# The forget gates' small logarithm chain on GpSimd, and the loads of the state-space tables on GpSimd's queue

## The chip, the cores and the metric

One Trainium2 chip; the kernel runs on one core of it. The metric is device time in microseconds (us) of one execution. Engines are named as in the profile: PE (TensorE, matmuls; PEld is its weight load), DVE (VectorE), ACT (ScalarE), POOL (GpSimd), SP (SyncE, which here only issues DMAs). An engine's name with a q (SPq, POOLq) is its instruction queue. L1820 is line 1820 of the kernel.

## The reference

Two transformer-like blocks on 512 tokens of 1024 features in float32. The change touches the token mixers of the second block, of which there are two (one per layer), and a helper that the first block uses once.

```python
def token_mixer(h, w_in, forget_b, ...):
    u, q, k, v, f, g_a, g_b = jnp.split(h @ w_in, cuts, axis=-1)
    y_ssm = s5_ssm(u, ...)                      # 32 groups of 16 features, 64 complex states each
    z_val, z_gate = jnp.split(gelu(y_ssm) @ glu_w, 2, axis=-1)
    y_a = z_val * sigmoid(z_gate)
    y_b = forgetting_attention(q, k, v, f + forget_b) @ attn_w_out   # 8 heads of 64
    return (sigmoid(g_a) * y_a + sigmoid(g_b) * y_b) @ w_out

def forgetting_attention(q, k, v, f_logit):
    cum = cumsum(log_sigmoid(f_logit), axis=1)   # 512 tokens x 8 heads
    s = q k^T / 8 + (cum_t - cum_s), causal; softmax; @ v
```

The logarithm that the diff touches is `log_sigmoid(x) = min(x, 0) - log(1 + exp(-|x|))`; `log(1 + e)` is a polynomial of `s = e / (2 + e)`.

## The kernel before

Products are taken in three parts (high x high, high x low, low x high) of float32 values split by ACT (L122, the high part) and DVE (L125, the low part). Weights come from DRAM as raw units (tile `wr`, at most 1 MB, two buffers), issued by SP at L132 in the order of the program; ACT and DVE split a unit into `wh` and `wl`, and PE uses it. A unit's DMA can be issued when the raw buffer that it takes has been split.

The instructions of SP stay in program order. Those of PE, DVE and ACT do so in the stages that are written out by hand (`down` and `up`; in the attention PE's alone); elsewhere, and for POOL everywhere, a planner at build time orders each engine's instructions by program order and by when it expects them to be ready. On the chip each engine executes its list in order, and waits at an instruction that isn't ready.

A mixer runs in this order:

1. The end of the feed-forward layer before it: `down`, the norms of four tiles of 128 tokens (each takes two POOL instructions, L294 and L297), transposes (tile `tp`, L340) and the first three blocks of the mixer's own projections, whose sums make `u`.
2. The scan stage, `ssm`. Sixteen tiles of states s, four for each feature tile j. For each s: products of the inputs with the table `b` (L1842, `bu`), a turn, a scan and a turn back on DVE (L1857 to L1875, which gives `st_x`), products with the tables `k` and `c` (L1878 and L1880, `st`), and four copies by ACT (L1882). Between them PE works on fourteen products of the gates (tile `gab`, L214 to L216), one after each of the first ten s, each unit of weights feeding two; ACT takes their sigmoid and stores it (L2076, L2077: `sga`, `pair`).
   `load(j)` fetches what feature tile j takes: four DMAs for `b` (128 KB each, L1820), one for `sc` (512 KB, L1821), four for `k` (tile `st_k`, 16 to 64 KB, L1824) and one for `c` (512 KB, L1825), ten in all, from DRAM, where the layers before have put them. Each tile has two buffers. `load(0)` is called ahead of the loop and `load(j + 1)` at the first s of j; after it `inputs(j + 1)` issues sixteen copies of `u` on POOL (L1834). The calls stand ahead of the next `take()` of weights in the program, so on SP they stand ahead of the weights' DMAs.
3. The attention. PE in this order: values of heads 4 to 7 with the forget logits f, queries and keys of the first two heads (`qk`), values of heads 0 to 3 (`v`, four token tiles in three PSUM buffers), the cumulative sum (`cum`, L1913, of `f_lf` with the triangle `tri`), then the heads one by one. `forget_logs` (L1899 to L1905) turns f into `f_lf`: tiles of 128 x 32, two ACT instructions (L1900, L1901) and 26 DVE instructions, most of them in `log1p` (L1063 to L1071).

The DMA of POOL's queue are generated by software; SP's and ACT's are the hardware kind (q1, q10 in the profile).

Of the kernel before, what the change touches and what calls it, by code (L numbers as in the profile page):

```python
# [44 lines left out]
class Builder:  # L45
# [14 lines left out]
    # ---------------------------------------------------------------- helpers  # L60
# [5 lines left out]
    def ring(self):  # L66
        """Room for two units of weights, for good."""
        p = self.late.enter_context(self.pool("weights", side="right"))
        self.wp, self.nw, self.used, self.kept = [p, p, None], 2, [0, 1, 2], []

    @contextmanager
    def third(self, side):
        """Room for a third unit."""
        with self.pool("third", side=side) as self.wp[2]:
            self.nw = 3
            yield
            self.nw = 2

    @contextmanager
    def psum_pool(self, **tags):  # L80
        """PSUM by tags: how many pairs of banks each; in a tag that ends in 1, single banks."""
        with self.tc.tile_pool(name="psum", bufs=1, space=PSUM, reuse_waits="tile") as p:
            old = getattr(self, "ps", None)
            self.ps = (p, tags)
            yield p
            self.ps = old
# [24 lines left out]
    def pair(self, name, tag):  # L111
        """Two banks that engines may use at the same time."""
# [5 lines left out]
    def split(self, src, h, l, eng="act"):  # L118
        """h + l = src exactly, both of twelve significant bits."""
# [7 lines left out]
    def load_w(self, pieces, n, chunks=1):  # L127
        """Stage one unit of weights (n words a partition); the function returned splits it."""
# [18 lines left out]
    def stage_cols(self, w, cols, k0=0, k1=None, chunks=1, dmas=1):  # L147
        """Columns of w (lists of (start, width)) for the row tiles k0..k1; a function gives them split, [p, k, column]."""
# [21 lines left out]
    def feed(self, units):  # L170
        """Queue functions that stage weights (or pairs of a name and a function), in the order of their use by take()."""
        self.units += [u if isinstance(u, tuple) else ((), u) for u in units]

    def take(self, *name, keep=False, hold=False):
        """The next queued weights; the ones after them come on their way (but for hold)."""
# [10 lines left out]
    def advance(self, keep=False):  # L186
        """Have two units ready or in work, if there is room beside those kept."""
# [9 lines left out]
    def stage(self, n):  # L197
        """Have n units of weights on their way."""
# [4 lines left out]
    def poke(self, n=1):  # L203
        """Split n parts of the weights that come next."""
# [13 lines left out]
    def fm(self, ps, wh, wl, c, kts=KD, xh=None, xl=None, t=slice(0, S), ks=None):  # L218
        """ps = w[:, c].T @ x, features x tokens (of the sum over kts tiles, those in ks)."""
# [9 lines left out]
    def tok(self, x, k, tt):  # L229
        """Features k x the tokens of tile tt."""  # L230
        return x[:, tt // 2, k, tt % 2 * P:(tt % 2 + 1) * P]

    def bg(self, steps=1, psum=True):
        """Advance the queued side work by some steps (without PSUM: what does not ask for PE next)."""
# [16 lines left out]
    # ---------------------------------------------------------------- setup  # L251
# [17 lines left out]
    def consts(self, part):  # L269
        """The constants that the first norm takes, or the others."""  # L270
# [13 lines left out]
    # ---------------------------------------------------------------- norms  # L284
    def norm_scale(self, srcs, junk, which):
        """1 / sqrt(mean(x ** 2) + eps) for each row of x, in one piece or in two."""
# [13 lines left out]
    def post_add(self, tt, acc, grow, out=None):  # L300
        """x[tt] += grow * acc / rms(acc), to out too; a generator of three stages."""
# [25 lines left out]
    def pre_steps(self, tt, src, scale, shift, xh=None, xl=None):  # L327
        """Norm of src (128 tokens), scaled and shifted, to features x tokens; a generator of four stages."""
# [30 lines left out]
    # ---------------------------------------------------------------- modulation  # L359
    def mod_sums(self, mp, l, i, order):  # L360
        """silu(c) @ mod_w for three vectors before the sum over partitions; a generator (None, or a vector when done)."""
# [22 lines left out]
    def mod(self, mp, l, i, which=(1, 0, 2)):  # L384
        """The modulation vectors of sublayer (l, i), as a generator."""
# [35 lines left out]
    def gate_row(self, l, i):  # L421
        """The gate of sublayer (l, i) along the free dimension of every partition."""
# [5 lines left out]
    # ---------------------------------------------------------------- products  # L428
# [5 lines left out]
    def down(self, kts, act, done, pre=None, last=4, bg=0):  # L434
        """tokens x D = act.T @ w, all of it in PSUM; done(tt, acc) as token tiles finish, then pre(tt).

        With pre, the first three blocks of the next product follow; returns their sums."""
# [111 lines left out]
    def split_act(self, pool, src, bufs=4):  # L549
        """A function of k that gives the split of src[:, k]."""  # L550
# [9 lines left out]
    def up(self, npair, evac, sums=()):  # L560
        """Blocks of 2 x 128 outputs, features x tokens; sums: the first ones, done already. A step of side work after each product."""
# [41 lines left out]
    def ffn(self, l, i, sums, mods):  # L603
        """Sublayer (l, i) of the second block: x += gate * norm(swiglu(pre(x)))."""
# [29 lines left out]
    # ---------------------------------------------------------------- first block  # L634
    def qstack(self, dst, ps, half):
        """dst rows 0..63 = high part and rows 64..127 = low part of ps rows of one half, times SCALE (a power of two)."""
# [5 lines left out]
    def kstack(self, kh, kl, ps, half):  # L642
        """kh = the high part of ps rows of one half, twice; kl = the low part, twice."""
# [7 lines left out]
    def rope(self, pool, z, tt, n):  # L651
        """Rotary embedding of the first 16 of each 64 columns; z has n blocks for each token tile in tt."""
# [24 lines left out]
    def stage_first(self, kind, n):  # L677
        """The weights of one product of the first block's mixer; columns of w_in or others."""
# [24 lines left out]
    def merge_gate(self, n, th, keep=False):  # L703
        """th = tanh(merge_g / 2) of two feature tiles; a generator of short products."""
# [11 lines left out]
    def merge_gates(self, fp):  # L716
        """The merge gates of the last two branches to DRAM; a generator of short products."""
# [7 lines left out]
    def compress_in(self, xp, zc, mh, ml):  # L725
        """The first norms, and the raw keys and values to compress, tokens first; the nsa gates."""
# [76 lines left out]
    def nsa_gates(self, zc, b1):  # L803
        """The three gates of each head, halved; tokens x 48."""
# [16 lines left out]
    def mem_kv(self, mh, ml):  # L821
        """Keys and values of mem, tokens first."""
# [29 lines left out]
    def compress_blocks(self, cp, zc, v, cp2=None):  # L852
        """The blocks of keys (or values) with their position, split."""
# [22 lines left out]
    def compress(self, b1, cp0, cp, zc, bk, mem, fill):  # L876
        """Compressed keys and values of the nsa branch."""
# [83 lines left out]
    def rnn(self, rp, fill):  # L961
        """The gated recurrence; y = (1 + tanh) y_rnn / 2, its merge gate's share; in two halves of the features."""
        nc, a, col = self.nc, self.a, self.col
        # 8 softplus(-lambda), by log1p(e) = 2 atanh(e / (2 + e))
# [4 lines left out]
        self.log1p(sp, e, s, s2)  # L969
# [51 lines left out]
        def scan(h):  # L1021
            y4 = self.y[:, 4 * h:4 * h + 4]
            nc.scalar.activation(y4, y4, AF.Gelu_apprx_tanh)
            for m in range(2):
                th = rp.tile([P, 2, S], F32, tag="th1", bufs=2, name="th1")
                nc.gpsimd.dma_start(th, self.mg[4 + 2 * h + m])
                for x in range(2):
                    n = 4 * h + 2 * m + x
                    t, y, (R, T, G) = th[:, x], self.y[:, n], RTG[n]
                    # sqrt(1 - a^2) = (1 + a) sqrt(tanh(-log(a) / 2))  # L1030
# [29 lines left out]
    def log1p(self, out, e, s, s2):  # L1060
        """out = log(1 + e) for 0 <= e <= 1 (e is lost)."""
        nc = self.nc
        nc.vector.tensor_scalar(s, e, 2.0, None, op0=OP.add)  # L1063
        nc.vector.reciprocal(s, s)
        nc.vector.tensor_tensor(s, s, e, op=OP.mult)
        nc.vector.tensor_tensor(s2, s, s, op=OP.mult)
        nc.vector.memset(e, 1.0 / 17.0)
        for d in (15, 13, 11, 9, 7, 5, 3, 1):
            nc.vector.tensor_tensor(e, e, s2, op=OP.mult)
            nc.vector.tensor_scalar(e, e, 1.0 / d, None, op0=OP.add)  # L1070
        nc.vector.scalar_tensor_tensor(out, s, 2.0, e, op0=OP.mult, op1=OP.mult)  # L1071

    def cross(self, cp, fill):
        """Attention over mem: y += (1 + tanh) y_x / 2."""
# [79 lines left out]
    def nsa_qkv(self, np_, g, out):  # L1154
        """Queries, keys and values of one group, and its compressed attention; a generator of short products."""
        nc = self.nc
        q = np_.tile([P, 4, S], F32R, tag="q", bufs=2, name="q")
        # the last group's waits have no other products to fill them: its values and probabilities stay unsplit
# [1138 lines left out]
```

## Time and profile before

| | us |
|---|---|
| median of 3 runs | 3304.46 (3300.73 to 3306.01) |
| span of the profiled execution, first to last instruction | 3298.7 |
| what lies around the span, taken as the median less the span | 5.8 |
| scan stage and start of the attention, first layer | 1446 to 1620 |
| scan stage and start of the attention, second layer | 2578 to 2750 |

The profile page gives each engine's busy time, the busy share in 40 slices, the DMA queues, a chain of waits and the costliest groups of instructions. The trace behind it can be asked for the instructions of a stretch in order of time, for waits by who ended them, and for busy time and granted PE clock in chosen stretches. All times within the trace count from the start of the span. The profiled execution's own device time is not listed beside the runs; its span stands for it.

### The profile page before, as it was taken

The page shows a single profiled execution, that of the slowest core. Times are in us where ns is not written, and L with a number is a line of the kernel's source. Part 1 is how long each engine was busy: PE and PEld are TensorE (multiplying, and loading weights), DVE is VectorE, ACT ScalarE, POOL GpSimd, SP SyncE. Part 2 cuts the span into 40 slices and gives each one's busy share as a digit, 9 for nine tenths or more (in the row PEclk, how much of TensorE's full clock was granted, in tenths as well). Part 3 has the DMA queues.
Part 4 walks back from the last instruction along what each step waited for, and adds up shares of the span by engine and source line. Part 5 has one row for each costly group of instructions (what it writes and reads, how often), then busy time and mean ns, then how long its engine had stood idle before and what let it go on. Part 6 is the DMA issues. An engine that isn't in the chain of part 4 may idle for free. (4 is left out here: it accounts for less than half of the span.)

```text
span 3298.7 us, 43184 instructions
## 1 busy us (share of the span) xinstructions
PE 3213.4 (97%) x16515; PEld 2677.0 (81%) x16515; DVE 1919.4 (58%) x3524; ACT 1433.0 (43%) x2991; POOL 318.0 (10%) x645
## 2 busy tenths in 40 slices
PE   8999999999999999998999999999999898999999
PEld 7878888698888888886788888898888777898887
DVE  7576777576655665466576564366645556752233
ACT  6465767545334222355454225342234455452232
POOL 0000000010101110021111110011101211100000
PEclk9999999999999999999999999999999999999999
DMA  5444211244433775465435464247743652533332
GB/s 184 116 129 132 52 39 39 77 141 159 137 130 109 212 236 178 107 135 130 100 119 183 133 200 129 102 128 231 236 140 100 166 120 79 182 106 90 102 103 77
DMA packets 412799, 434.47 MB, mean 132 GB/s; under 512 B 34816, under 2 KB 349360, under 8 KB 412592
## 3 DMA queue, kind: packets, MB, share of 16 engines
q1 hardware_dynamic: 372288, 297.45, 32.2%
q0 software_dynamic: 32816, 116.43, 10.7%
q10 hardware_dynamic: 7488, 17.83, 1.4%
q8 instruction: 130, 2.13, 0.3%
q14 instruction: 77, 0.63, 0.1%
HBM read 395.46 MB, written 36.20 MB: 131 GB/s over the span
## 5 line engine op out<-in xcount | busy, mean ns | idle before, releaser
L125 DVE TENSOR_TENSOR wl<-wr,wh 128x512 fp32r<-128x512 f32 (+2 forms) x940 | 667.5, 739 | 391.1 <-ACT wh L122 389.1
L214 PE MATMUL up<-x_h,wh 128*128 128x512 f32 (+1 forms) x2096 | 750.3, 358 | 0.0
L215 PE MATMUL up<-x_l,wh 128*128 128x512 f32 (+1 forms) x2096 | 745.3, 356 | 0.0
L216 PE MATMUL up<-x_h,wl 128*128 128x512 f32 (+1 forms) x2096 | 744.8, 355 | 0.0
L122 ACT CAST wh<-wr 128x512 fp32r<-128x512 f32 (+2 forms) x940 | 570.2, 661 | 231.8 <-DMA wr<-in_mix_w_in_dram 83.8
L214 PEld LDWEIGHTS up<-x_h,wh 128*128 128x128 f32 x2096 | 393.5, 188 | 59.3 <-issue 1.6
L216 PEld LDWEIGHTS up<-x_h,wl 128*128 128x128 f32 x2096 | 393.3, 188 | 59.5
L215 PEld LDWEIGHTS up<-x_l,wh 128*128 128x128 f32 x2096 | 393.9, 188 | 56.6 <-DVE x_l L125 0.2
L447 PE MATMUL acc<-wh,ah 128*128 128x512 f32 x1152 | 381.4, 393 | 1.0 <-DVE merged L2148 1.0
L451 PE MATMUL acc<-wh,al 128*128 128x512 f32 x1152 | 379.0, 391 | 0.9 <-DVE al L125 0.9
L449 PE MATMUL acc<-wl,ah 128*128 128x512 f32 x1152 | 379.7, 392 | 0.0
L612 ACT ACTIVATE sg<-up 128x512 f32<-128x512 f32 x88 | 52.6, 598 | 523.2 <-PE up L216 272.7
L125 DVE TENSOR_TENSOR al<-hid,ah 128x512 fp32r<-128x512 f32 x120 | 82.6, 691 | 325.8 <-ACT ah L122 325.7
L451 PEld LDWEIGHTS acc<-wh,al 128*128 128x128 f32 x1152 | 216.2, 188 | 49.4 <-DVE al L125 1.3
L447 PEld LDWEIGHTS acc<-wh,ah 128*128 128x128 f32 x1152 | 216.3, 188 | 48.2 <-DVE merged L2148 1.8
L449 PEld LDWEIGHTS acc<-wl,ah 128*128 128x128 f32 x1152 | 216.4, 188 | 47.0
L122 ACT CAST ah<-hid 128x512 fp32r<-128x512 f32 x120 | 74.0, 620 | 367.4 <-PE acc L449 346.0
L378 DVE SCALAR_TENSOR_TENSOR macc<-wm,silu_c,macc 128x1024 f32<-128x1024 f32 x126 | 161.1, 1278 | 12.7 <-DMA wm<-in_mod_w_dram 12.6
L614 DVE TENSOR_TENSOR hid<-up,sg 128x512 f32<-128x512 f32 x88 | 60.7, 689 | 149.9 <-PE up L216 149.6
L369 POOL DMA_DIRECT2D wm<-in_mod_w_dram x144 | 77.4, 538 | 441.0 <-DVE macc L378 253.9
L294 POOL TENSOR_SCALAR nv<-nv 128x1 f32<-128x1 f32 x58 | 18.2, 313 | 1013.2 <-ACT junk L292 862.1
L214 PE MATMUL gab<-x_h,wh 128*128 128x512 f32 x224 | 93.5, 417 | 0.0
(544 smaller groups left out, 5301.4 us busy)
## 6 DMA issues: line engine op xcount, KB each, us to landing
wr<-in_ffn_w_in_dram SPq DMA_DIRECT2D x176, 512.0 KB, 5.3
wm<-in_mod_w_dram POOLq DMA_DIRECT2D x144, 512.0 KB, 5.1
wr<-in_ffn_w_out_dram SPq DMA_DIRECT2D x44, 1024.0 KB, 4.9
wr<-in_mix_w_in_dram SPq DMA_DIRECT2D x48, 512.0 KB, 10.7
wr<-in_w_in_dram SPq DMA_DIRECT2D x17, 1024.0 KB, 5.3
wr<-in_w_up_dram SPq DMA_DIRECT2D x16, 1024.0 KB, 5.5
wr<-in_w_down_dram SPq DMA_DIRECT2D x16, 1024.0 KB, 4.9
wr<-in_w_in_dram SPq DMA_DIRECT2D x16, 512.0 KB, 5.3
```

The costliest lines, as they stand in the source:

```text
L122: nc.scalar.copy(h, src)
L125: nc.vector.tensor_tensor(l, src, h.bitcast(F32), op=OP.subtract)
L214: nc.tensor.matmul(ps, lh, rh, start=start, stop=False, **kw)
L215: nc.tensor.matmul(ps, lh, rl, start=False, stop=False, **kw)
L216: nc.tensor.matmul(ps, ll, rh, start=False, stop=stop, **kw)
L369: nc.gpsimd.dma_start(raw, src[:, k, (3 * i + w) * D:(3 * i + w + 1) * D])
L378: nc.vector.scalar_tensor_tensor(acc, raw, s, acc, op0=OP.mult, op1=OP.add)
L447: nc.tensor.matmul(acc[tt][q], ah[:, t], wh[:, q * 512:(q + 1) * 512], start=first, stop=False)
L449: nc.tensor.matmul(acc[tt][q], ah[:, t], wl[:, q * 512:(q + 1) * 512], start=False, stop=False)
L451: nc.tensor.matmul(acc[tt][q], al[:, t], wh[:, q * 512:(q + 1) * 512], start=False, stop=final)
L612: nc.scalar.activation(sg, ps[0], AF.Silu)
L614: nc.vector.tensor_tensor(hid[:, n], ps[1], sg, op=OP.mult)
```

## The change

`log1p` takes the engine that its arithmetic runs on; the reciprocal stays on DVE. `forget_logs` passes GpSimd, and its other DVE instructions go to GpSimd too. In the first block's `rnn` the helper stays on DVE. The last step, one DVE instruction `(s * 2) * e`, becomes two instructions on either engine. In `ssm` the ten DMAs of each `load(j)` are issued from GpSimd's queue rather than SP's; their order, sizes and buffers stay. Two mixers call each, so 80 DMAs move. The rest of the diff empties comment lines and docstrings and moves no line.

```diff
-        self.log1p(sp, e, s, s2)
+        self.log1p(sp, e, s, s2, nc.vector)
...
-    def log1p(self, out, e, s, s2):
-        """out = log(1 + e) for 0 <= e <= 1 (e is lost)."""
-        nc = self.nc
-        nc.vector.tensor_scalar(s, e, 2.0, None, op0=OP.add)
-        nc.vector.reciprocal(s, s)
-        nc.vector.tensor_tensor(s, s, e, op=OP.mult)
-        nc.vector.tensor_tensor(s2, s, s, op=OP.mult)
-        nc.vector.memset(e, 1.0 / 17.0)
+    def log1p(self, out, e, s, s2, eng):
+
+        eng.tensor_scalar(s, e, 2.0, None, op0=OP.add)
+        self.nc.vector.reciprocal(s, s)
+        eng.tensor_tensor(s, s, e, op=OP.mult)
+        eng.tensor_tensor(s2, s, s, op=OP.mult)
+        eng.memset(e, 1.0 / 17.0)
         for d in (15, 13, 11, 9, 7, 5, 3, 1):
-            nc.vector.tensor_tensor(e, e, s2, op=OP.mult)
-            nc.vector.tensor_scalar(e, e, 1.0 / d, None, op0=OP.add)
-        nc.vector.scalar_tensor_tensor(out, s, 2.0, e, op0=OP.mult, op1=OP.mult)
+            eng.tensor_tensor(e, e, s2, op=OP.mult)
+            eng.tensor_scalar(e, e, 1.0 / d, None, op0=OP.add)
+        eng.tensor_tensor(e, e, s, op=OP.mult)
+        eng.tensor_scalar(out, e, 2.0, None, op0=OP.mult)
...
             for m in range(CH):
-                nc.sync.dma_start(b[32 * m:32 * m + 32].rearrange("r q x n -> r q (x n)"), bd[m])
-            nc.sync.dma_start(sc, self.turns[l][:, 4 * j:4 * j + 4])
+                nc.gpsimd.dma_start(b[32 * m:32 * m + 32].rearrange("r q x n -> r q (x n)"), bd[m])
+            nc.gpsimd.dma_start(sc, self.turns[l][:, 4 * j:4 * j + 4])
             for m in range(CH):
                 o = 32 * (CH - 1 - m)
-                nc.sync.dma_start(k[32 * m:32 * m + 32, :, o:], kd[:, :, :P - o])
-            nc.sync.dma_start(c, self.sm_c[l][j].rearrange("p (x s n) -> p x s n", x=2, s=4))
+                nc.gpsimd.dma_start(k[32 * m:32 * m + 32, :, o:], kd[:, :, :P - o])
+            nc.gpsimd.dma_start(c, self.sm_c[l][j].rearrange("p (x s n) -> p x s n", x=2, s=4))
...
-        nc.vector.tensor_tensor(z, f, fb[:, None, :].to_broadcast([P, NT, 8]), op=OP.add)
+        nc.gpsimd.tensor_tensor(z, f, fb[:, None, :].to_broadcast([P, NT, 8]), op=OP.add)
         nc.scalar.activation(e, z, AF.Abs)
         nc.scalar.activation(e, e, AF.Exp, scale=-1.0)
-        self.log1p(l1, e, s, s2)
-        nc.vector.tensor_scalar(z, z, 0.0, None, op0=OP.min)
+        self.log1p(l1, e, s, s2, nc.gpsimd)
+        nc.gpsimd.tensor_scalar(z, z, 0.0, None, op0=OP.min)
         for o in (0, 32):
-            nc.vector.tensor_tensor(lf[:, :, o:o + 8], z, l1, op=OP.subtract)
+            nc.gpsimd.tensor_tensor(lf[:, :, o:o + 8], z, l1, op=OP.subtract)
```

## Rows read from the trace of the kernel before

**Rows 1.** The page, its first part: busy us, share of the span, instructions.
```profile
PE 3213.4 (97%) x16515; PEld 2677.0 (81%) x16515; DVE 1919.4 (58%) x3524; ACT 1433.0 (43%) x2991; POOL 318.0 (10%) x645
```

**Rows 2.** PE's waits, 1400 to 1620 and 2580 to 2750: total us, times, longest.
```profile
PE st L1880 <- DVE st_x L1874: 12.2, 2, 9.4
PE bu L1842 <- DMA b<-ssm_b: 6.8, 1, 6.8
PE v L214 <- DVE v L125: 6.6, 1, 6.6
...
PE st L1880 <- DVE st_x L1874: 10.1, 2, 9.9
PE v L214 <- DVE v L125: 9.0, 1, 9.0
PE bu L1842 <- DMA st_k<-ssm_k: 5.8, 1, 5.8
```

**Rows 3.** SP's instructions in order of time, 1439 to 1505: start, us, what.
```profile
1439.68 0.99 SPq L132 DMA_DIRECT2D wr<-in_mix_w_in_dram  x2
1440.84 6.58 SPq L1820 DMA_DIRECT2D b<-ssm_b  x4
...
1467.38 1.06 SPq L132 DMA_DIRECT2D wr<-in_mix_w_in_dram  x2
1485.50 1.75 SPq L1820 DMA_DIRECT2D b<-ssm_b  x4
...
1492.31 12.58 SPq L132 DMA_DIRECT2D wr<-in_mix_w_in_dram  x4
```

**Rows 4.** SP's own waits, 1400 to 1700: total us, times, longest.
```profile
SPq L1820 <- DMA pair<-sg: 18.3, 2, 17.0
```

**Rows 5.** ACT in order of time, at the longest stall of the first scan stage.
```profile
1510.29 1.04 ACT L122 CAST wh<-wr 128x1024 fp32r<-128x1024 f32 x1 [15.04 <-DMA wr<-in_mix_w_in_dram]
```

**Rows 6.** Stretches: us, busy by engine, granted PE clock, DMA share, GB/s.
```profile
1518.00:1520.00 2.00, 2.00 (x7) 1.71 (x7) 2.00 (x3) 1.32 (x4) 0.00 (x0) 0.50 0.87 293
1520.00:1522.00 2.00, 2.00 (x9) 1.55 (x9) 1.93 (x7) 1.97 (x3) 0.00 (x0) 0.86 0.83 197
```

**Rows 7.** DMA issues: KB each, median us from issue to landing.
```profile
wr<-in_ffn_w_in_dram SPq DMA_DIRECT2D x176, 512.0 KB, 5.3
...
wr<-in_mix_w_in_dram SPq DMA_DIRECT2D x48, 512.0 KB, 10.7
```

**Rows 8.** POOL's groups of instructions: busy us, mean ns, idle before.
```profile
L369 POOL DMA_DIRECT2D wm<-in_mod_w_dram x144 | 77.4, 538 | 441.0 <-DVE macc L378 253.9 <-DVE macc L376 155.5 <-DMA wm<-in_mod_w_dram 23.4
...
L297 POOL TENSOR_TENSOR ny<-nv,mhalf 128x1 f32<-128x1 f32 x62 | 37.0, 596 | 5.0
...
L1290 POOL TENSOR_TENSOR smx<-smx,gates 128x4 f32<-128x4 f32 x32 | 8.2, 257 | 152.0 <-DVE smx L1288 143.3 <-ACT q L639 4.4 <-ACT th L711 2.2
```

**Rows 9.** POOL in order of time, from the last norm on; idle before in brackets.
```profile
1420.94 0.29 POOL L294 TENSOR_SCALAR nv<-nv 128x1 f32<-128x1 f32 x1 [3.60 <-ACT xn L292]
1421.32 0.55 POOL L297 TENSOR_TENSOR ny<-nv,mhalf 128x1 f32<-128x1 f32 x1
...
1454.00 0.65 POOL L2092 DMA_DIRECT2D gl_sg<-sga  x1 [5.92 <-issue]
...
1476.83 7.50 POOL L1834 COPY u<-u 32x128 f32<-32x128 f32 x16 [10.79 <-PE st L1878]
1508.08 9.11 POOL L1834 COPY u<-u 32x128 f32<-32x128 f32 x16 [23.74 <-issue]
```

**Rows 10.** PE in order of time, the last norm's transposes and the cumulative sum.
```profile
1422.88 1.03 PE L340 MATMUL tp<-cst_t,xn 128*128 128x128 f32 x8
...
1612.04 2.66 PE L1913 MATMUL cum<-tri,f_lf 128*40 128x512 f32 x8
```

**Rows 11.** DVE in order of time, the forget chain of the first layer.
```profile
1596.46 0.18 DVE L1063 TENSOR_SCALAR f_s<-f_e 128x32 f32<-128x32 f32 x1 [0.32 <-ACT f_e L1901]
...
1607.43 0.29 DVE L1905 TENSOR_TENSOR f_lf<-f_z,f_l 128x32 f32<-128x32 f32 x2
```

## The prediction, made before the changed kernel ran

> **What bounds the kernel now.** I read the page's busy times first: PE is busy for 97% of the span [rows 1], so only stretches in which PE waits, or runs at its lower clock, can be won. Next I asked for PE's waits in the two mixers, where the change lies. The reader is to see five long ones in the scan stages and two at the start of the attentions [rows 2]. In the scan stages they make 6.8 + 12.2 (two waits, of 2.8 and 9.4) + 5.8 + 10.1 (9.9 nearly alone) = 34.9 us; before the values of the attention 6.6 + 9.0 = 15.6 us. The rest of this text is about those seven waits.
>
> What is behind them? The first wait of each scan stage is put down to a table's DMA. The second kind is put down to DVE's `st_x`, but that is only the last link: at the longest of them ACT sat 15.04 us at the cast of a weight that hadn't landed until 1510.29, with the copies out of PSUM queued behind it [rows 5]. So I looked at when SP issued that weight, in SP's order of time. Four `b` tables start at 1440.84 and hold the queue for 6.58 us; the next weights go out at 1467.38; then nothing until `b` of the third feature tile at 1485.50, and weights again only at 1492.31 [rows 3]. SP's waits name what stood in front: 17.0 us at L1820, a table load [rows 4]. It was waiting for a store of ACT's, which no data of `b` depends on; I read it as a limit on what is under way in the hardware queues, and for the sum it matters only that a table load blocked SP while weights stood behind it.
>
> Each stall costs more than its idle time. After the one of 9.4 us PE's granted clock is 0.50 in the first full stretch of 2 us and 0.86 in the next [rows 6], the lower of its two levels (1.2 GHz) and a return to 2.4. That is 2.0 x 0.50 + 2.0 x 0.14 = 1.3 us of work lost in these two stretches, which I count for each of the five: 6.5 us.
>
> **The tables on GpSimd's queue.** SP loses 80 DMAs, so weights are issued when their raw buffer is free. POOL gains them, ten for each of four loads in each of two layers. What an issue costs there: 0.538 us, the mean of 144 loads, up to 0.65 us beside a split of DVE's [rows 8, 9]. So ten cost 5.4 to 6.5 us. The bytes and the sixteen DMA engines stay.
>
> For the first two loads of a layer both buffers are free, and POOL has little to do before the scan stage but the norms; SP reaches these loads only at 1440.84, behind weights that wait for their buffers. I expect some or all of the twenty to be issued before that, and to land before the stage begins. Then the weight issued at 1439.68 competes with less. Its landing takes between the 5.3 us of a like transfer in the feed-forward layers and the 10.7 us that is the median for this tensor [rows 7], thus 1445.0 to 1450.4, and a cast of about 1 us and DVE's half follow. What is left of the first wait is then between nothing and about 4 us; I take 2. For the later waits the unit issued at 1492.31 can go out as soon as the split before it has freed its buffer, at least the 17.0 us earlier that SP stood at L1820, against a wait of ACT's of 15.04. I take 2 us left there as well. Bounds for the five together: nothing won (the transfers are as late as now) and 34.9 + 6.5 = 41.4 us won. Taken: 41.4 - 5 x 2 = 31.4 us.
>
> **What the loads stand in front of on POOL.** Behind a load's ten issues stand sixteen copies of `u`, 7.50 to 9.11 us, and stores and loads of the gates. A round of POOL is then 13 to 16 us. The copies of two successive feature tiles start 31.3 us apart now (1476.83 and 1508.08) [rows 9], 28.5 without the 2.8 us stall between them; so the copies are hidden, until an issue takes about (28.5 - 8.3) / 10 = 2.0 us.
>
> The norms aren't hidden. The last one's two POOL instructions run from 1420.94 to 1421.87 after 3.60 us of idleness, DVE scales the tile, and PE transposes it at 1422.88 [rows 9, 10]; a delay there goes to PE almost one for one. The planner may place table loads in the gaps. If it fills them up, a norm waits for the rest of one issue, 0 to 0.65 us; if all twenty stand ahead of the last norm, 20 x 0.65 - 3.6 = 9.4 us a layer. I take 1 us a layer, nearer the lower end, because the gap alone holds six issues: -2 us.
>
> **The forget chain on GpSimd.** On DVE it runs from 1596.46 to 1607.72 among splits and evacuations [rows 11]: 24 instructions that stand between DVE and the values PE waits for. Without them I get, from DVE's other instructions in that stretch, a restart of PE some 3 us earlier in each layer, not 6.6, since the weight splits and the keys stay ahead of the values. POOL has no row for 128 x 32 arithmetic. Bounds for one instruction: 0.257 us (tensor by tensor, 128 x 4) and 0.596 us (a power, 128 x 1) [rows 8]. Between, the start-to-start time of two dependent POOL instructions, 0.38 us [rows 9], is nearest, for it has the same kind of dependence. After the reciprocal come 23 of them, counting the split last step: 5.9, 8.7 or 13.7 us. With 1.2 us for going to DVE's reciprocal and back (an estimate: 0.35 of DVE's work and two hand-overs) and about 2.9 us of POOL's own casts of queries and keys among them, `f_lf` is there at 1596.5 + 1.2 + 8.7 + 2.9 = 1609.3 (1606.5 to 1614.3). PE starts the cumulative sum at 1612.04 now [rows 10], and would reach it at about 1609. So the chain is just in time: I take 3 us for each layer, 6 together. Bounds: 2 x 2.3 = 4.6 us lost, and 15.6 + 2 x 1.3 = 18.2 us won if the whole wait goes. In `rnn` one DVE instruction of 128 x 8 more is under 0.3 us once, beside PE's products: nothing, 0.3 if it has no cover.
>
> **Sum.** 31.4 - 2 + 6 = 35.4 us: a span of 3298.7 - 35.4 = 3263.3 us. The median of the runs is 5.8 us above the profiled span, which gives 3269 us.
>
> **Rivals.** *The transfers are the limit, not their order.* For it: the DMA share is 0.87 and 0.83 just after the long stall [rows 6], and the same bytes must pass. Against it: SP stood still for 17.0 us with weights behind it. With half of the idle time left and the lower clock after it: 17.4 won, 2 lost at the norms, nothing at the attention: 3304.5 - 15.4 = 3289 us. The Trainium skill, DMA: Bandwidth & Descriptors, section Rules for kernel authors, states that spreading DMAs over queues gives no bandwidth, as all run on the same sixteen engines, and saves issue time alone; by that rule it is this rival as far as the stalls are transfer time.
>
> *The forget chain becomes PE's wait.* At the upper price PE waits for `f_lf` to 1614.3: 2.3 us lost a layer and nothing won, 3269 + 6 + 4.6 = 3280 us.
>
> *POOL becomes the bound of the scan stage, and the kernel slower.* It decides from 2.0 us an issue on. At 3.0 us a round takes 30 + 8.3 = 38.3 us against 28.5, and the two later rounds of each layer come 9.8 us late: 4 x (9.8 + 1.3) = 44.4 us. With 3 us more at each layer's norms, and the 31.4 and 6 us still won: 3304.5 + 44.4 + 6 - 37.4 = 3317 us. Against it: no issue is near that in 0.538 and 0.65 us [rows 8, 9]. The Trainium skill, SBUF — State Buffer, sections A bandwidth-pool intuition that's wrong and Who interferes with whom, says that a DVE copy with two ports shuts GpSimd out while it writes descriptors, and gives 620 ns that become 3100 ns; the trace's 0.65 us beside a DVE instruction doesn't bear that out for a split.
>
> *The change doesn't do what it says:* the planner puts the loads on POOL where SP had them, and the time stays at 3304 us.
>
> **Chances.** Forecast 0.55; transfers 0.17; forget chain 0.13; POOL bound 0.10; no effect 0.05. 0.2%, about 6.6 us, is what a measurement of this kernel can tell from no change. Faster: the first three, less 0.02 for a weaker transfer case, 0.83; same 0.06; slower 0.11. The range goes down to all that could be won (41.4 + 18.2 = 59.6, 3245 us, where I stop at 3247) and up past the transfer rival to 3298 us; outside are the slower case, no effect and the last of the low end, just under 0.2.
>
> **What would show it.** Right: SP's waits at L132 name splits alone, table DMAs on POOLq start before 1440, PE's wait at `bu` is under 3 us and the waits of 9 us at `st` are gone, with the clock at 1.00 across the stage. The wait at `v` falls to about 3 us, and a short one may appear at `cum`. Wrong: `wr` landings of over 15 us with a full DMA share (transfers); idle time ahead of `tp`, or norms with POOL's issues in front (norms); `bu` waiting for `u` or a table late in a round (POOL bound); `cum` waiting for `f_lf` past 1612.

## The result, and the profile after

The changed kernel takes 3268.24 us (median of 4 runs, 3267.44 to 3271.33) against 3303.75 us for the kernel before (4 runs beside it, 3300.73 to 3306.01): a ratio of 0.9894 with a 95% interval of 0.988 to 0.9908. The profiled execution took 3267.97 us, its span is 3266.2 us. The forecast was 3269 us. So the number came out. The rest of this text asks whether it did for the reasons given, and for the largest term it did so only in part.

PE's waits after the change, in the two mixers (the lines answer to [rows 2]; total us, times, longest):

```profile
PE st L1880 <- DVE st_x L1874: 5.1, 1, 5.1
PE s L1966 <- ACT kb L1921: 2.4, 1, 2.4
PE v L214 <- DVE v L125: 1.6, 1, 1.6
PE tp L340 <- DVE xn L335: 1.2, 3, 0.8
...
PE st L1880 <- DVE st_x L1874: 5.5, 1, 5.5
PE v L214 <- DVE v L125: 3.7, 1, 3.7
PE s L1966 <- ACT kb L1921: 1.3, 1, 1.3
PE tp L340 <- DVE xn L335: 1.2, 3, 0.8
```

Both waits at `bu` are gone, and so are the waits of 9.4 and 9.9 us. One wait of 5 us a layer is left in the scan stages, at the first state product; a short one is new at the scores (`s`). Scan stages: 34.9 us of idleness before, 5.1 + 5.5 = 10.6 after. Attentions: 15.6 before, 1.6 + 3.7 + 2.4 + 1.3 = 9.0 after. The norms pay 1.2 us a layer.

SP in order of time, as in [rows 3]:

```profile
1451.68 0.99 SPq L132 DMA_DIRECT2D wr<-in_mix_w_in_dram  x2
1456.91 8.24 SPq L132 DMA_DIRECT2D wr<-in_mix_w_in_dram  x2
1475.89 15.28 SPq L132 DMA_DIRECT2D wr<-in_mix_w_in_dram  x4
```

Between the weights at 1439.68 and the next ones at 1467.38 stood 27.7 us; now the pairs follow each other at 1451.68, 1456.91 and 1475.89. SP issues nothing but weights from 1386 to 1518, and no wait of its own in the scan stages names a table or a store. POOL in order of time shows where the tables went:

```profile
1413.50 1.21 POOL L1820 DMA_DIRECT2D b<-ssm_b  x2
...
1418.37 1.08 POOL L294 TENSOR_SCALAR nv<-nv 128x1 f32<-128x1 f32 x1
...
1425.79 1.65 POOL L1820 DMA_DIRECT2D b<-ssm_b  x3
...
1433.92 0.56 POOL L1821 DMA_DIRECT2D sc<-turns  x1 [3.61 <-DMA st_k<-ssm_k]
...
1439.18 0.56 POOL L1825 DMA_DIRECT2D c<-ssm_c  x1 [0.20 <-issue]
...
1489.66 1.21 POOL L1824 DMA_DIRECT2D st_k<-ssm_k  x2 [7.55 <-DMA gl_sg<-sga]
```

The twenty issues of the first two loads lie between 1413.50 and 1439.74, among the last norms and just behind them, and ahead of 1440.84, where SP began them before [rows 3]. Note the brackets: POOL too stands still for a transfer that the table has nothing to do with, 7.55 us for `gl_sg`. This will matter.

### The profile page after: what moved, and what is told of

Same layout as the page of the kernel before. It is cut to its first block, busy times and chain, and to the rows that moved or that the text cites. A ratio compares the mean times of both kernels' runs of the same rounds, so it can differ in the third digit from the quotient of the medians.

```text
span 3266.2 us, 43186 instructions
## 1 busy us (share of the span) xinstructions
PE 3208.3 (98%) x16515; PEld 2672.8 (82%) x16515; DVE 1907.8 (58%) x3475; ACT 1433.3 (44%) x2991; POOL 379.3 (12%) x777
## 3 DMA queue, kind: packets, MB, share of 16 engines
q0 software_dynamic: 37680, 130.33, 12.2%
## 4 chain that ended last, share of the span: by engine, by line
PE 87%; DVE 4%; ACT 4%; DMA 3%; issue 1%; POOL 1%; SPq 0%; ACTq 0%; DVEq 0%; POOLq 0%
PE up L214 12%; PE up L216 12%; PE up L215 12%; PE acc L451 8%; PE acc L449 8%; PE acc L447 8%; DMA wr<-in_mix_w_in_dram 3%; PE gab L216 1%; PE gab L214 1%; PE gab L215 1%; PE o L1435 1%; DVE wl L125 1%; PE pt L1315 1%; PE zvg L214 1%; PE zvg L216 1%; PE zvg L215 1%
## 5 line engine op out<-in xcount | busy, mean ns | idle before, releaser
L294 POOL TENSOR_SCALAR nv<-nv 128x1 f32<-128x1 f32 x58 | 19.4, 335 | 1010.8 <-ACT junk L292 866.0
```

## What stands behind SP's wait

The prediction saw SP wait 17.0 us at a table load [rows 4], called it a limit on what is under way, and took it for a table that stood in front of weights. The program says more. This is its list of SP's instructions before the change, with the semaphores that each waits for (numbers in names left out; `DMAHW0` to `7` count landings of SP's and ACT's DMAs, `DMASW` those of POOL's, and the other names count an engine's instructions):

```
191 L1824 DMA st_k<-ssm_k 32x4x32 [waits DMAHW7,DMASW4,Pool]
192 L1824 DMA st_k<-ssm_k 32x4x64 [waits DMAHW1]
193 L1824 DMA st_k<-ssm_k 32x4x96 [waits DMAHW2]
194 L1824 DMA st_k<-ssm_k 32x4x128 [waits DMAHW3]
195 L1825 DMA c<-ssm_c 128x1024 [waits DMAHW4,DMASW1]
196 L132 DMA wr<-in_mix_w_in 128x8x128 [waits DMAHW5,DVE]
197 L132 DMA wr<-in_mix_w_in 128x8x128 [waits DMAHW6]
198 L1820 DMA b<-ssm_b 32x4x256 [waits DMAHW0,DMASW4,PE]
```

The numbers run round from 0 to 7; those that SP leaves out, the 0 between rows 191 and 192 among them, are ACT's stores. So there are eight places, SP and ACT share them in turn, and a DMA goes out only when the one eight before it has landed: row 198, a table, waits for a store of ACT's. POOL's DMAs have eight places of their own (`DMASW`). This is the store in the trace before the change, and what the four stores to that tensor from 1440 to 1520 took to land (shortest, median, longest):

```profile
1470.04 0.33 ACTq L2077 DMA_DIRECT2D pair<-sg  x1
...
DMA to landing us min/median/max: 3.2/5.4/15.4
```

Issued at 1470.04 and 15.4 us under way, it landed at 1485.44, and SP's next issue is that of 1485.50 [rows 3]. That gives two rivals to the prediction's reading, which stands first:

- **Order** (the prediction): a table stood in front of weights in SP's queue; off the queue, the weights go out earlier.
- **Places**: tables use up the eight places, so anything in them waits for ACT's slow stores, weights too; on POOL they use others.
- **Early landing**: what counts is that the first tables pass before the stage begins.

## Experiments

Each kernel was timed in five rounds beside the kernel before on the same chip; ratios are to that, with 95% intervals.

**The two parts by themselves.** `e1_tables` is the kernel before with the ten issues of `load` on `nc.gpsimd`; `e2_chain` is the changed kernel with these on `nc.sync` again.

```diff
# e1_tables: this and the other three dma_start of load(), log1p as before
-                nc.sync.dma_start(b[32 * m:32 * m + 32]...
+                nc.gpsimd.dma_start(b[32 * m:32 * m + 32]...
```

> Only the tables' loads go to GpSimd's queue; the logarithm stays on VectorE. If the two parts of the change add up as the trace after suggests (the first layer's scan stage ends 14.9 us earlier, the second's another 11.8 us), this kernel takes 26.7 us off: about 3277 us, with PE's waits at bu and the 9.4 and 9.9 us at st gone. My prediction's own terms say 31.4 - 2 = 29.4 us, 3274. Rival: the time between the attention's values and its sums was won by earlier weights and not by the chain; then this kernel alone gives the whole change, 3268 us. Second rival, the transfers are the limit: no more than 15 us, 3289.

Measured: 3277.53 us, 0.9921 (0.9909 to 0.9934).

> Only the forget gates' logarithm goes to GpSimd; the tables stay on SyncE's queue. If the chain is worth what the prediction says, 3 us a layer, this gives 3298 us; the trace after (22.3 us earlier at the cumulative sum, 18.3 behind the scores, against 14.9 ahead of the attention) says 3.4 us in the first layer and 2.4 in the second, 3298 as well. Rival: the gain at the attention came from weights that landed earlier, or what the chain wins is given back at the keys and queries: 3304 us, and PE waits as long at the scores as it no longer does at v.

Measured: 3293.16 us, 0.9974 (0.9962 to 0.9985). The parts add up: 25.3 + 9.7 = 35.0 us against 35.5 for both. The chain alone won more than the 6 us expected, but its six executions lie between 3290.93 and 3299.29 us, and the traced one took 3298.59. The rival that weights, not the chain, freed the attention is out: with the tables alone PE still waits 7.0 and 9.2 us at `v`, with the chain alone 1.7 and 5.2. First layer, `e1_tables` and `e2_chain`:

```profile
PE v L214 <- DVE v L125: 7.0, 1, 7.0
...
PE v L214 <- DVE v L125: 1.7, 1, 1.7
```

**Half of the loads each.** `e3_late_pool` puts the first two loads of a layer back on SP, `e4_early_pool` the last two.

```diff
             k = ks[j % 2]
+            eng = nc.gpsimd if j > 1 else nc.sync      # e4: the other way round
...
-                nc.gpsimd.dma_start(b[32 * m:32 * m + 32]...
+                eng.dma_start(b[32 * m:32 * m + 32]...
```

> As the change, but the first two loads of each layer go back to SyncE's queue; the last two stay on GpSimd's. If what counts is that the later tables no longer block SyncE with weights behind them, little is lost: the first stall is 5.1 and 5.5 us in the changed kernel against 6.8 and 5.8 at bu before, 2 us together, and about 1 us a layer comes back at the norms: 3268 us within 4. If the early landing of the first tables carries its part, as the prediction's terms say (6.8 and 5.8 us and 1.3 us of lower clock at each), this kernel is about 11 to 15 us slower than the change: 3279 to 3283 us.

Measured: 3301.48 us, 0.9991 (0.9982 to 1.0).

> As the change, but the last two loads of each layer go back to SyncE's queue; the first two stay on GpSimd's. If the later tables on SyncE make the long stalls, these come back (2.8 + 9.4 and 9.9 us idle and 1.3 us of lower clock at each of three): 26 us slower than the change, 3294 us. Rival: SyncE is blocked only because all four loads are on its queue, or the early landing of the first two is what frees the transfers: 3268 to 3275 us.

Measured: 3295.97 us, 0.9982 (0.9973 to 0.9991). Both contain the chain, which alone gives 3293.16 us, 0.9974. So either half of the tables on POOL wins nothing beyond it; together they win 25 us. For e3 both theories were far off; for e4 the first came out (3294 us expected). PE's waits in e3, first layer, and SP's:

```profile
PE st L1881 <- DVE st_x L1875: 12.9, 2, 8.6
PE bu L1843 <- DMA b<-ssm_b: 6.2, 1, 6.2
...
SPq L132 <- DMA pair<-sg: 19.0, 1, 19.0
```

No table of the later loads is on SP here, and yet a stall of 8.6 us is there. It is a weight (L132) that waits 19.0 us for ACT's store: the twenty early tables hold the weights back until 1468.88, and the place of the next one is then the store's. In e4 the later tables are on SP:

```profile
SPq L1821 <- PE bu L1843: 17.9, 1, 17.9
...
PE st L1881 <- DVE st_x L1875: 12.8, 3, 6.3
```

There a table of the third tile waits 17.9 us for its own buffer, which PE's `bu` is still reading, with weights behind it. That is the prediction's case, order, but by another wait than the one it had read. (The traced execution of e4 took 3289.68 us, the shortest of eleven.)

**Weights in front, tables on SP.** `e6_sp_behind` is the kernel before with the call of `load(j + 1)` behind `fill(s)`.

```diff
-                if q == 0 and j < 3:
-                    nxt = load(j + 1), inputs(j + 1)
...
                 fill(s)
+                if q == 0 and j < 3:
+                    nxt = load(j + 1), inputs(j + 1)
```

> The kernel before, with all tables on SyncE's queue, but each later load asked for behind the scan step's product instead of ahead of it, so that in SyncE's program two weights more stand in front of the third load and two in front of the fourth. Theory of the prediction: a table load stood in front of the weights and blocked them; then the stalls of 9.4 and 9.9 us and the lower clock behind them shrink by most of their 22 us, 3283 us. Second theory: in the program a DMA of SyncE or ScalarE first waits until the one eight places before it, of either of the two, has landed, so whatever stands in that place waits for ScalarE's store, and the tables fill those places in any order; then the weights wait as long in front as behind, 3303 us within 6.

Measured: 3302.76 us, 0.9996 (0.9988 to 1.0005). SP's wait and PE's:

```profile
SPq L132 <- DMA pair<-sg: 16.4, 1, 16.4
...
PE st L1878 <- DVE st_x L1872: 13.2, 2, 10.8
```

The wait has moved from the table to the weight that took its position, and nothing is won. Order alone is refuted for the kernel before; places stand.

**ACT's stores on POOL, tables on SP.** `e7_stores_pool` is the kernel before with the stores of the gates issued from POOL's queue.

```diff
-            nc.scalar.dma_start(pair[n][:, 0] if g else sga[n], t)
+            nc.gpsimd.dma_start(pair[n][:, 0] if g else sga[n], t)
```

> The kernel before, with the tables on SyncE's queue, but ScalarE's stores of the gates go to GpSimd's queue. Second theory (eight places shared by SyncE and ScalarE): SyncE's wait of 17.0 us for a store goes and the stalls of 9.4 and 9.9 us shrink, while the first stalls of 6.8 and 5.8 us stay: 3282 to 3292 us. Theory of the prediction (the twenty tables between two weights are what holds the weights): only the later stall's part that is due to the store goes, 3296 us or more. Rival to both: GpSimd, which takes its work in order, holds the stores behind the copies of u, a gate's buffer comes free late and PE waits there: 3304 us or more.

Measured: 3289.08 us, 0.9956 (0.9944 to 0.9969), without touching a table. PE's waits, first and second layer:

```profile
PE st L1880 <- DVE st_x L1874: 8.7, 2, 6.7
PE bu L1842 <- DMA b<-ssm_b: 5.9, 1, 5.9
...
PE st L1880 <- DVE st_x L1874: 4.7, 1, 4.7
```

SP no longer waits for any store, the later stalls fall from 12.2 to 8.7 and from 10.1 to 4.7 us, the first ones stay (5.9 and 6.0). In the trace before, ACT shows no wait at these stores, so it is SP that gains. Places are shown to be worth about 15 us here (10 to 18.5 by the interval). The rest of the 25 I put down to the early tables, which still pass ahead of the weights on SP; no run has both the stores and the early tables off it.

**Early landing.** `e9_hold` holds the second load of each layer on POOL until `u`'s second tile is there.

```diff
+            if j == 1:
+                for t in (b[:, 0, 0, 0:1], sc[:, 0, 0, 0:1], k[:, 0, P - 1:], c[:, 0, 0, 0:1]):
+                    nc.gpsimd.tensor_copy(t, u[:, 1, 0:1])
             for m in range(CH):
```

> The changed kernel, but the second load of each layer is held until the second tile of u is there (four small copies of GpSimd write into its tables first), some 15 us later than now. If the first stalls that are left (5.1 and 5.5 us) come from these early tables, which pass with the weights of the first scan step, they fall to 1 to 2 us and the lower clock behind them goes: 3268 - 2 x (4 + 1.3) = 3258 us. Rival: the bytes are only moved into the stage, the next weights land late and the stall comes two or three steps later, or the second load itself is late for its tile: 3268 us or more, up to 3280.

Measured: 3281.88 us, 0.9933 (0.9921 to 0.9946), 13.6 us slower than the change. Its stall at the first state product, by layer:

```profile
PE st L1883 <- DVE st_x L1877: 11.6, 1, 11.6
...
PE st L1883 <- DVE st_x L1877: 14.1, 1, 14.1
```

My expectation had the sign wrong: the ten tables then pass from 1443 on, beside the weights of the first scan step, and 5.1 and 5.5 us become 11.6 and 14.1. ACT shows the link in the first layer, a weight that landed late:

```profile
1457.97 1.05 ACT L122 CAST wh<-wr 128x1024 fp32r<-128x1024 f32 x1 [10.31 <-DMA wr<-in_mix_w_in_dram]
```

So it matters that the early tables have landed before the stage begins.

**How near POOL is to being the bound.** `e8_split_dma` cuts each table's DMA in two.

```diff
-                nc.gpsimd.dma_start(b[32 * m:32 * m + 32]..., bd[m])
+                for h in (0, 2):
+                    nc.gpsimd.dma_start(b[32 * m:32 * m + 32, h:h + 2]..., bd[m][:, h:h + 2])
# and so for sc, k and c
```

> The changed kernel with each table's DMA cut in two: the same bytes in twice as many issues on GpSimd's queue, twenty a load. By the prediction's point (2.0 us for each of ten issues before GpSimd becomes the bound) 20 x 0.56 = 11.2 us a load is still hidden, and only the norms lose about 1 us more a layer: 3270 us. Rival: GpSimd's queue has eight places of its own, the twenty wait for landings of 7 to 12 us, about 20 / 8 x 9 = 22 us a load, which with 8.3 us of copies exceeds the 28.5 us of a round by 2 us, and the norms are held up too: 3275 to 3290 us.

Measured: 3284.73 us, 0.994 (0.9927 to 0.9954), 16.5 us slower than the change, as the rival had it. POOL in order of time, and PE's waits in the first layer:

```profile
1437.35 0.57 POOL L1827 DMA_DIRECT2D st_k<-ssm_k  x1 [7.17 <-DMA sc<-turns]
...
PE st L1885 <- DVE st_x L1879: 8.7, 1, 8.7
PE tp L340 <- DVE xn L335: 5.3, 3, 4.9
```

An issue is still 0.56 us; what costs is POOL's own eight places (7.17 us for a table eight before) and a norm behind them (4.9 us at `tp`). The second layer is alike: 8.7 us at `st` and 5.6 at `tp`. These waits make 28.3 us in the two layers against 13.0 in the changed kernel, most of the 16.5.

**What is left at the first stall.** `e10_first_table` leaves out the loads of the second to fourth tiles (all tiles take the first tile's tables). `e11_one_b` stores `b` so that one DMA loads it; `e12_one_b_order` also puts `b`, `sc` and `c` ahead of the clearing of `k`; `e13_fill_first` is that with the first gate product ahead of the first state product.

```diff
# e10_first_table
         cur, nxt = load(0), None
+        load = lambda j: cur
# e11_one_b (and four stores of 32 rows in ssm_static)
+            nc.gpsimd.dma_start(b.rearrange("p q x n -> p (q x n)"), self.sm_b[l][j])
# e12_one_b_order: c's dma_start ahead of k's, and there
+            if j < 2:
+                nc.gpsimd.memset(k, 0.0)
# e13_fill_first, behind pb = states(s + 1, cur[0], v)
+                if not s:
+                    fill(s)
```

> The changed kernel with the second, third and fourth load of each layer left out (the tables of the first feature tile serve all four, so the scan's numbers are others): 5.1 MB a layer less. It bounds what the transfers still cost. If the first stalls that are left (5.1 and 5.5 us) are the second load passing beside the first weights, they go: 3268 - 2 x (5 + 1.3) = 3255 us, and the later steps win nothing, since no long wait is left there. Rival: the first stall is the first load's, or has nothing to do with tables: 3264 to 3268 us.

Measured: 3262.75 us, 0.9881 (0.9864 to 0.9897).

> The changed kernel with table b laid out in DRAM as the scan takes it, so that it comes in one DMA of 4 KB rows and not in four of 1 KB rows: the same bytes, seven issues a load and not ten (the table's store is cut in four for it, earlier in the program). Second theory (places and early landing): the first two loads are through some 3 to 5 us earlier, the first stalls of 5.1 and 5.5 us become 2 to 3: 3260 to 3264 us. If only bytes count: 3268 us.

Measured: 3269.34 us, 0.9904 (0.9889 to 0.9919).

> As the kernel with b in one DMA, and in the program the tables b, sc and c stand ahead of the clearing of k, so that GpSimd issues three of them in the idle 5.6 us between two norms that the changed kernel left empty (1406.5 to 1412.1) and the twenty end some 10 us earlier. If the first stall is the early tables beside the weights issued at 1420.60 to 1428.52, it is gone or under 1 us: 3268 - 2 x (5 + 1.3) = 3255 us. If it has another cause, 3264 to 3268 us; if the norms are held up by the issues, 1 to 3 us more.

Measured: 3264.68 us, 0.9889 (0.9875 to 0.9904).

> As the kernel with b in one DMA and the tables ahead of the clearing of k, and the first gate product of the scan stage stands ahead of the first state product in TensorE's order. In the traces so far the first stall of some 5 us stays even where the later tables are left out: TensorE has done fifteen of that gate's 24 products and waits for st_x, whose chain on VectorE began only behind a weight split. If that is its cause, the nine products that are left (2 us) can run in it as soon as the second split is done: the stall falls from 5 to about 3 us in each layer, 2 x 2 us and some of the lower clock won: 3260 us. Rival: the split that the nine products need ends no earlier than st_x, and the order makes no difference: 3265 us.

Measured: 3268.25 us, 0.9903 (0.9886 to 0.9919). PE's first stall in e10 and in e13, first layer:

```profile
PE st L1881 <- DVE st_x L1875: 4.5, 1, 4.5
```

```profile
PE st L1882 <- DVE st_x L1876: 3.5, 2, 2.6
```

Four misses, and the first three came out near their rival. Without 5.1 MB of tables a layer the stall is still 4.5 us, and with all early issues done by 1423.93 (e12) it is 4.8: it is no longer, in the main, a transfer of tables. The changed kernel's DVE, in order of time, and then its PE:

```profile
1453.86 1.22 DVE L125 TENSOR_TENSOR wl<-wr,wh 128x1024 fp32r<-128x1024 f32 x1 [2.21 <-ACT wh L122]
1455.00 0.42 DVE L1857 TENSOR_TENSOR rot_a<-bu,sc 128x256 f32<-128x256 f32 x1
...
1458.76 0.29 DVE L1874 TENSOR_TENSOR st_x<-rot_a,rot_b 128x128 f32<-128x128 f32 x1
```

```profile
1459.11 1.22 PE L1880 MATMUL st<-st_x,c 128*128 128x128 f32 x4 [5.11 <-DVE st_x L1874]
```

DVE starts the scan's chain at 1455.00, behind a weight split that waited for ACT's cast, and the chain with a second split in it takes 4.0 us. What made the split late isn't shown. ACT's cast of a weight had waited for its landing just before, in the changed kernel (the weight ahead of this one) and in e10 (this one):

```profile
1448.21 2.18 ACT L122 CAST wh<-wr 128x512 fp32r<-128x512 f32 x4 [6.13 <-DMA wr<-in_mix_w_in_dram]
```

```profile
1452.68 1.05 ACT L122 CAST wh<-wr 128x1024 fp32r<-128x1024 f32 x1 [4.37 <-DMA wr<-in_mix_w_in_dram]
```

So late weights stay a candidate for what is left. In e13 the stall shrank as expected, to 2.6 + 0.9, and the time didn't; where that went isn't known. None of the four is told apart from the change (0.9894) by its interval, so no better version is claimed.

## Why the forecast came out, step by step

**The long stalls (term of 31.4 us).** The size was near: with the 2 us at the norms the prediction had 29.4, and the tables alone measured 25.3 (22 to 30 by the interval). The mechanism was half right. "A table load blocked SP while weights stood behind it" was the step that failed: with the weights put in front (e6) the weight waits in the same place, and with the later tables off SP (e3) too. What the runs show in its place is three things that hold weights back. One is a place that a slow store of ACT's has taken; freeing the places alone wins 15.2 us with all tables still on SP (e7). One is a table that waits in SP's queue for its own buffer, 17.9 us in e4; that is order, but not the wait that was read. One is tables that pass while the stage runs; ten of the first twenty late cost 13.6 us (e9). The whole change takes away the first two and has the first twenty tables ahead of the stage. The prediction had two of them in view (the limit, and "land before the stage begins") but priced the stalls one by one; e3 and e4 show that they can't be added, as each half wins nothing.

**What is left of the stalls (5 x 2 us).** The sum of 10 is 10.6, but it lies in one wait of 5.1 and one of 5.5 us, and the last link is DVE's chain behind a split, not a late table.

**The lower clock (1.3 us a stall).** Too small for one stall, near in the sum. Stretches after the stall of 5.1 us in the changed kernel (columns as in [rows 6]):

```profile
1458.00:1460.00 2.00, 0.89 (x5) 0.89 (x5) 1.86 (x6) 0.00 (x0) 0.00 (x0) 0.50 1.01 57
1460.00:1462.00 2.00, 2.00 (x7) 1.61 (x7) 1.93 (x7) 1.55 (x4) 0.00 (x0) 0.50 1.03 104
1462.00:1464.00 2.00, 2.00 (x9) 1.63 (x8) 0.57 (x3) 0.12 (x1) 0.00 (x0) 0.67 1.08 291
```

0.89 x 0.50 + 2.0 x 0.50 + 2.0 x 0.33 = 2.1 us were lost there; the prediction had left out the first, partial stretch. Two stalls are left, so the net counts. The page after the change has, against [rows 1]:

```profile
PE 3208.3 (98%) x16515; PEld 2672.8 (82%) x16515; DVE 1907.8 (58%) x3475; ACT 1433.3 (44%) x2991; POOL 379.3 (12%) x777
```

PE is busy for 3213.4 - 3208.3 = 5.1 us less with the same 16515 instructions. I put that down to the clock, and no run separates it; the prediction had 6.5 for all five stalls. Its sign that the clock stays at 1.00 across the stage did not come: the mean of the first scan stage rose from 0.92 to 0.97. In the waits shown, PE's idleness fell by 24.3 + 6.6 - 2.2 (the norms) = 28.7 us; with the 5.1 that is 33.8, against 32.5 by which the span fell.

**The norms (2 us).** Right: PE's wait at `tp` is 1.2 us in each layer, where it was 0.2 at most, and with the tables alone 1.0 and 1.2.

**The forget chain (6 us).** Right in the first layer, by its own working. POOL there, and PE at the sum:

```profile
1575.35 0.32 POOL L1062 TENSOR_SCALAR f_s<-f_e 128x32 f32<-128x32 f32 x1 [1.22 <-ACT f_e L1901]
...
1577.28 0.25 POOL L1068 TENSOR_TENSOR f_e<-f_e,f_s 128x32 f32<-128x32 f32 x1
1577.62 0.30 POOL L1069 TENSOR_SCALAR f_e<-f_e 128x32 f32<-128x32 f32 x1
...
1581.75 2.55 POOL L1068 TENSOR_TENSOR f_e<-f_e,f_s 128x32 f32<-128x32 f32 x1
...
1588.34 0.46 POOL L1905 TENSOR_TENSOR f_lf<-f_z,f_l 128x32 f32<-128x32 f32 x2
```

```profile
1589.78 2.35 PE L1913 MATMUL cum<-tri,f_lf 128*40 128x512 f32 x8
```

From the first instruction to the last 13.4 us, where the prediction had 1.2 + 8.7 + 2.9 = 12.8; a pair of instructions takes 0.72 us from start to start, 0.36 each, where 0.38 was taken. `f_lf` ends 1.0 us ahead of `cum`: just in time, as forecast. In the second layer the chain took 19.4 us, from 2684.79 on, because POOL stood 7.12 us inside it at a cast of a query; PE came to the sum later too, and `f_lf` still ended 2.5 us ahead of `cum`. The wait at `v` fell by 5.0 and 5.3 us, more than the 3 foreseen, and 2.4 and 1.3 came back, not at `cum` but one step later, at the scores:

```profile
1593.63 2.00 ACT L122 CAST wh<-wr 128x1024 fp32r<-128x1024 f32 x2 [3.37 <-DMA wr<-in_mix_w_in_dram]
```

```profile
1595.85 0.68 DVE L1917 TENSOR_SCALAR f_t<-cum 40x512 f32<-40x512 f32 x1
```

The sum is there at 1592.1, but DVE takes it only at 1595.85, behind the split of that late weight. 5.0 + 5.3 - 3.7 = 6.6 us net in the trace, 9.7 (5 to 13 by the interval) in e2.

**Around the span (5.8 us).** Wrong: that was mostly the spread of the runs. The changed kernel's execution has 3267.97 - 3266.2 = 1.8 us there, and later executions of the kernel before about 2. With 2 us, the span of 3298.7 belongs to an execution like the fastest of its runs (3300.73), not to the median. The span came out 2.9 us above the 3263.3 of the sum, the surroundings some 4 us below; the two errors cancel. So do those of the two parts: the tables won 4.1 us less than the 29.4 forecast and the chain 3.7 more than its 6, as far as the intervals tell. That 3269 stands so near to 3268.24 is luck to that extent.

**The rivals.** *Transfers are the limit*: no. The bytes are the same, and leaving out three loads in four (e10) wins 5.5 us more, within what the intervals leave open. When they pass matters (e9). The Trainium skill, DMA: Bandwidth & Descriptors, section Rules for kernel authors, has that more queues bring no bandwidth but issue time alone. The trace agrees on the bandwidth: the DMAs moved 147 GB/s in the first scan stage before and 143 after. What was won here was not issue time either, it was places to wait in and earlier landings. *Forget chain as PE's wait*: no, by 1.0 us. *POOL as the bound*: not in this kernel, but its point of 2.0 us an issue was far too generous. e8 loses 16.5 us at 2 x 0.56 = 1.1 us for each former issue, because POOL's places and the norms were left out of that sum. *No effect*: no, the early issues begin at 1413.50.

## What to carry to other kernels

When a queue waits for a transfer that its instruction has nothing to do with, look in the program for what the two share, here a ring of eight completion counters, before pricing it as order; the test is to put something else in that position. A gain that rests on several conditions can show nothing when half of the change is tried, so try the whole before dropping an idea, and don't add up stalls that are one backlog. Prefetches on an idle engine's queue paid here by landing before the busy stage. The number of DMAs counts there too: cutting each in two made that engine stall in its own ring and cost half of the gain, while joining four of ten into one won nothing that the interval shows.

## What the runs showed of the hardware that was not expected

A store of 256 KB by ACT took 15.4 us to land when it was issued just behind twenty tables and two weights; the median of the four to that tensor is 5.4 us. POOL's 128 x 32 arithmetic is 0.25 us (two tensors) and 0.29 to 0.32 us (a tensor and a number), 0.36 us from start to start in a chain. One such instruction took 2.55 us at 1581.75, in the same 2.3 us in which DVE ran two splits of 128 x 1024 (1581.84, 2.34 us). The second layer repeats it, as shown below; the other fourteen instructions of this line in the two layers take 0.25 to 0.26 us. That DVE's split held POOL up is an inference from these two.

```profile
2697.20 2.54 POOL L1068 TENSOR_TENSOR f_e<-f_e,f_s 128x32 f32<-128x32 f32 x1
```

```profile
2697.28 2.35 DVE L125 TENSOR_TENSOR wl<-wr,wh 128x1024 fp32r<-128x1024 f32 x2
```
